# FFN output in two passes with six of eleven pairs by seven products, and retention's queries by seven products

## Chip, core and metric

The kernel runs on one core of one Trainium2 chip. Its time is the device time of one execution in microseconds, over 3 runs: median 1178.73, lowest 1178.39, highest 1178.78. The engines are named as in the profile: PE (TensorE matmul), PEld (its weight load), DVE (VectorE), ACT (ScalarE), POOL (GpSimd), SP (SyncE, which issues most transfers).

## What is computed

One decoder layer on 512 tokens and 16 meta tokens, width 1024: normalisation, a combined projection, retention (4 heads) beside stick-breaking attention (16 heads), an output projection, and a SwiGLU FFN of 2816 columns. The change is in the queries of retention and in the last product of the FFN. The core of the reference there:

```python
proj = hn @ w_in
rq, rk, rv, rg, sq, sk, sv, ga, gb = jnp.split(proj, ..., axis=-1)
q_r = rotary(heads(rq, RET_HEADS), pos) * (RET_DK ** -0.5)
k_r = rotary(heads(rk, RET_HEADS), pos)
...
def swiglu(hn, w_ffn_in, w_ffn_out):
    a, b = jnp.split(hn @ w_ffn_in, 2, axis=-1)
    return (jax.nn.silu(a) * b) @ w_ffn_out
...
ff = swiglu(rmsnorm(h, norm_ffn_pre[l]), w_ffn_in[l], w_ffn_out[l])
h = h + rmsnorm(ff, norm_ffn_post[l])
return h[:, N_META:]
```

## The kernel before

**Products in three parts.** Every fp32 matrix is split into a high part (fp32r, made by ACT) and a low part (what the high part leaves, by DVE): `split` (L104, L101). A product of matrices is then three matmuls, high by high, high by low, low by high. A weight block comes from HBM into a `raw` tile (4 of them), and its two parts into `wh` and `wl` tiles (5 each, used in rotation).

**Seven products.** Much of the kernel multiplies 2x2 blocks of matrices by seven block products instead of eight (Strassen's scheme in Winograd's form): `PRODUCTS` names them a11, a12, a22 and s1 to s4 for the weights' blocks and their sums, b11 to b22 and t1 to t4 for the activations'. POOL makes the sums into `st` tiles (2 of them), `seven` runs the products and puts them together from the banks of PSUM. FFN-in (up to 1050.9 us) does so: per pair of row blocks of the FFN's 22 it runs 168 matmuls of 256 columns.

**Retention** (335 to 745 us) goes head by head. `ret_qk(h)` loads the head's 256 query columns as two units, computes the queries by 2 x 8 x 3 = 48 matmuls of 512 columns into two banks, rotates them (DVE reads the banks, ACT and DVE split the results), then loads and computes the keys with 96 matmuls of 264 columns. Scores, values and the state follow.

**FFN-out** (from 1050.9 us) multiplies the gated activations `gt`, which stand in SBUF as 11 pairs (`gt[:, f2]`, each four blocks of 256), with `w_ffn_out`. For each of 22 row blocks it splits 512 columns of `gt` and 1024 of the weights, and for each of 4 token tiles and 2 column halves runs three matmuls of 512 columns into one of 8 banks: 528 in all. The last four row blocks (`REST`) are run token tile by token tile, in the written order (`pinned`). So a token tile ends early: its squares (ACT), the power (POOL), the scaling and the last addition (DVE) and its transfers go beside the next tile's matmuls, and only the last tile's stand behind the last matmul. FFN-out's sums per bank stay in PSUM through all 22 row blocks.

**Order.** The instructions of an engine run in the order in which a list scheduler put them, at build time, by its own costs and the order of the code; matmuls and transfers under `pinned` stay as written. A tile that is used again waits until its last reader is done.

## Time and profile before

| what | value |
|---|---|
| median of the runs | 1178.73 us (1178.39 to 1178.78) |
| the profiled execution | 1178.72 us |
| its span | 1176.9 us |
| granted clock of PE | 0.999 |
| busy: PE, DVE, ACT, POOL | 99%, 72%, 45%, 28% |
| POOL in FFN-out up to 1149 us | 0 of 95 us |

The profile is of one execution. Busy time is the union of an engine's instructions; PE counts as busy through stretches in which matmuls follow each other at their spacing, which is shorter than the time that a row gives for one of them (they overlap). The spacing is read from the chain of waits, which gives stretches of one kind with their length and number. "L95 x24" is 24 instructions of line 95. `128x256` is partitions by elements.

### The profile page before, as it was taken

To read this page: it belongs to the slowest core of one execution; us is meant where nothing else is said; L and a number is where in the kernel's file an instruction comes from. 1 tells how busy PE (TensorE), PEld (TensorE's weight loads), DVE (VectorE), ACT (ScalarE), POOL (GpSimd) and SP (SyncE) were. 2 spreads that over 40 slices of the span, in tenths; PEclk is the share of its full clock that TensorE was granted. 3 is DMA by queue.
4 is the path that set the end of the run, shared out by engine and by line. 5 is a ranking of instruction groups with operands and counts; after the bars stand their busy time and mean duration, and the time that the engine had idled before them with its cause. 6 is when DMAs were issued, how large, how long until landed. Compare 5 with 4: busy or idle time off the path is not lost.

```text
span 1176.9 us, 18856 instructions
## 1 busy us (share of the span) xinstructions
PE 1164.9 (99%) x7529; PEld 1056.3 (90%) x7529; DVE 844.0 (72%) x1120; ACT 532.1 (45%) x899; POOL 333.5 (28%) x358
## 2 busy tenths in 40 slices
PE   9999999999999999999999999999999999999997
PEld 7988999988899998998899898888999999998886
DVE  7488888888577873786586567767799998773333
ACT  6476666666233434434243334335455444442321
POOL 2021112126644403320240200001356676610000
PEclk9999999999999999999999999999999999999999
DMA  7332122222641323115122434344033333353311
GB/s 235 99 99 74 62 72 64 77 77 92 194 148 60 93 90 114 55 53 154 36 82 82 133 90 134 126 160 126 19 108 108 109 108 108 108 162 101 97 36 72
DMA packets 146536, 118.25 MB, mean 100 GB/s; under 512 B 3832, under 2 KB 135168, under 8 KB 146448
## 3 DMA queue, kind: packets, MB, share of 16 engines
q1 hardware_dynamic: 145856, 115.85, 32.5%
q8 instruction: 59, 0.97, 0.4%
q10 hardware_dynamic: 592, 1.20, 0.3%
q14 instruction: 29, 0.24, 0.1%
HBM read 109.96 MB, written 7.08 MB: 99 GB/s over the span
## 4 chain that ended last, share of the span: by engine, by line
PE 92%; DVE 5%; issue 1%; ACT 1%; DMA 0%; POOL 0%; POOLq 0%; DVEq 0%; ACTq 0%
PE pp L95 41%; PE pb L95 20%; PE pa L95 20%; PE pc L95 5%; PE px L95 3%; PE pb L98 3%; DVE wl L101 1%; DVE sm L603 1%; ACT wh L104 1%; DVE sl L101 0%; DMA ysb<-in_x_dram 0%; DVE al L101 0%; DVE kl L101 0%; DVE qb L101 0%; DVE qa L101 0%
## 5 line engine op out<-in xcount | busy, mean ns | idle before, releaser
L101 DVE TENSOR_TENSOR wl<-raw,wh 128x1024 fp32r<-128x1024 f32 x196 | 260.7, 1338 | 60.3 <-ACT wh L104 59.3
L104 ACT ACTIVATE wh<-raw 128x1024 fp32r<-128x1024 f32 x194 | 195.2, 1014 | 203.4 <-PE pa L95 59.5
L95 PE MATMUL pp<-hT,wh 128*128 128x512 f32 (+1 forms) x304 | 112.0, 369 | 0.0
L95 PE MATMUL pp<-hL,wh 128*128 128x512 f32 (+1 forms) x304 | 107.7, 354 | 0.0
L95 PE MATMUL pp<-hT,wl 128*128 128x512 f32 (+1 forms) x304 | 107.6, 354 | 0.0
L258 POOL TENSOR_TENSOR st<-raw 128x512 f32<-128x512 f32 x28 | 44.4, 1608 | 170.3 <-DMA raw<-in_w_in_dram 170.3
L101 DVE TENSOR_TENSOR wl<-st,wh 128x1024 fp32r<-128x1024 f32 x54 | 75.1, 1392 | 13.1 <-ACT wh L104 12.1
L95 PE MATMUL pp<-qk,wh 128*128 128x512 f32 x256 | 80.1, 394 | 0.0
L230 POOL TENSOR_TENSOR st<-raw 128x512 f32<-128x512 f32 x40 | 61.1, 1528 | 50.3 <-DVE wl L101 50.3
L95 PE MATMUL pp<-wh,hT 128*128 128x256 f32 (+1 forms) x240 | 73.9, 309 | 0.1
L95 PE MATMUL pp<-wl,hT 128*128 128x256 f32 (+1 forms) x240 | 73.0, 305 | 0.7 <-DVE wl L101 0.4
L95 PE MATMUL pp<-wh,hL 128*128 128x256 f32 (+1 forms) x240 | 73.0, 305 | 0.2 <-DVE hL L101 0.2
L104 ACT ACTIVATE wh<-st 128x1024 fp32r<-128x1024 f32 x54 | 56.6, 1056 | 35.6 <-PE pp L95 15.6
L95 PE MATMUL pa<-hL,wh 128*128 128x264 f32 (+1 forms) x208 | 66.2, 318 | 0.0
L95 PE MATMUL pa<-hT,wh 128*128 128x264 f32 (+1 forms) x208 | 66.2, 318 | 0.0
L95 PE MATMUL pa<-hT,wl 128*128 128x264 f32 (+1 forms) x208 | 66.1, 318 | 0.0
L603 DVE TENSOR_TENSOR_SCAN sm<-sm,mask 128x528 f32<-128x528 f32 (+1 forms) x64 | 54.8, 857 | 14.3 <-ACT sm L600 13.5
L95 PEld LDWEIGHTS pp<-hT,wl 128*128 128x128 f32 x304 | 57.2, 188 | 8.4
L613 POOL CAST mg<-sp 128x32 fp32r<-128x32 f32 x32 | 7.5, 233 | 197.6 <-DVE sp L604 153.7
L95 PEld LDWEIGHTS pp<-hT,wh 128*128 128x128 f32 x304 | 57.3, 188 | 5.8
L95 PEld LDWEIGHTS pp<-hL,wh 128*128 128x128 f32 x304 | 57.4, 189 | 5.3
L95 PEld LDWEIGHTS pp<-qk,wh 128*128 128x128 f32 x256 | 47.7, 188 | 10.7
(346 smaller groups left out, 3680.3 us busy)
## 6 DMA issues: line engine op xcount, KB each, us to landing
raw<-in_w_in_dram SPq DMA_DIRECT2D x88, 512.0 KB, 4.2
raw<-in_w_ffn_in_dram SPq DMA_DIRECT2D x44, 512.0 KB, 3.8
raw<-in_w_ffn_out_dram SPq DMA_DIRECT2D x22, 512.0 KB, 3.6
raw<-in_w_ret_out_dram SPq DMA_DIRECT2D x16, 512.0 KB, 3.4
raw<-in_w_sb_out_dram SPq DMA_DIRECT2D x8, 512.0 KB, 3.9
raw<-in_w_out_dram SPq DMA_DIRECT2D x8, 512.0 KB, 4.0
ysb<-in_x_dram SPq DMA_DIRECT2D x4, 512.0 KB, 7.1
gb_d<-go SPq DMA_DIRECT2D x8, 256.0 KB, 2.0
```

The lines of the kernel that those rows point to most:

```text
L95: return keep(nc.tensor.matmul(*args, **kw))
L98: return keep(nc.tensor.transpose(dst, src, idn))
L101: return nc.vector.tensor_tensor(lo, src, hi.bitcast(F32), op=ALU.subtract)
L104: ins = nc.scalar.activation(hi, src, AF.Copy)
L230: ins = nc.gpsimd.tensor_tensor(d, p, q, op=op)
L258: nc.gpsimd.tensor_tensor(d[:, k : k + 2], p[:, k : k + 2], q[:, k : k + 2], op=op)
L603: nc.vector.tensor_tensor_scan(rev, rev, mask[:, r0:][:, ::-1], 0.0, op0=ALU.mult, op1=ALU.max)
L613: nc.gpsimd.tensor_copy(g[:, two, 0:NM], m)
```

## The change

**Retention's queries.** `feat_quarters` loads the head's query weights in quarters and makes four sums of 512 columns on POOL; `feat_chain` runs seven products of 4 x 3 matmuls with 256 columns. Products that are only added up are chained in one bank: a11, s2, s3, a22 in the first, s1, s4 in the second, a12 in the third, with copies by ACT in between. The keys of the first half stand between the products. The result lies in SBUF, from where `rotate` reads it now.

**FFN-out.** It runs in two passes, one for each half of the 1024 output columns, and in steps `n` = 0 to 21: 0 to 10 are pass 0 with the pairs 0 to 10, 11 to 21 are pass 1 with the pairs 10, 9, 8, 7, 6, 5, 4, 3, 1, 2, 0. An odd pair is plain: 24 matmuls of 512 columns in a step. An even pair goes by seven products, 7 x 2 x 3 = 42 matmuls of 256 columns. `prepare(n)` loads a 256x512 weight block; for a seven pair POOL makes four sums of weights and three of activations, 256 columns each (and once per pair the difference t1 in place of b12), and ACT and DVE split raw weights and activations (1024 columns each), sums of weights and sums of activations (768 each). Pairs 10 and 8 keep their split activations for pass 1. The banks are put together into `y` after pass 0 (`combine`) and after pass 1. At the end the two seven pairs n=20 and 21 are run product by product, with the plain n=19 around them.

```diff
--- before.py
+++ after.py
@@ -139,13 +139,13 @@
...
-    def feat_mm(dst, unit, xh, xl, kn=KD):
+    def feat_mm(dst, unit, xh, xl, kn=KD, first=True, **kw):
...
+            mm(dst, wh[:, k, :], xh(k), start=(first and k == 0), stop=False, **kw)
+            mm(dst, wh[:, k, :], xl(k), start=False, stop=False, **kw)
+            mm(dst, wl[:, k, :], xh(k), start=False, stop=(k == kn - 1), **kw)
...
+    def feat_chain(u, tok, q, u22, beside=None):
...
+        def product(name, bank, more=False):
+            a, b = name
+            feat_mm(banks[bank], u[a], *tok.operand(b), KH, first=not more, skip_group_check=True)
...
+        def add(d, p):
+            nc.vector.tensor_tensor(d, p, d, op=ALU.add)
...
+        (q11, q12), (q21, q22) = [[q[:, e, H * t : H * (t + 1)] for t in range(2)] for e in range(2)]
+        def rest():
+            banks["c"] = bank_p()[:, :H]
+            product(("a12", "b21"), "c")
+            add(q11, banks["c"])
+        banks["a"] = bank_a()[:, 0, :H]
+        product(("a11", "b11"), "a")
+        nc.scalar.activation(q11, banks["a"], AF.Copy)
+        if beside:
+            rest()
+        banks["b"] = bank_p()[:, :H]
+        product(("s1", "t1"), "b")
+        nc.scalar.activation(q22, banks["b"], AF.Copy)
+        product(("s2", "t2"), "a", True)
+        nc.scalar.activation(q12, banks["a"], AF.Copy)
+        product(("s4", "b22"), "b", True)
+        add(q12, banks["b"])
+        product(("s3", "t3"), "a", True)
+        nc.scalar.activation(u22, banks["a"], AF.Copy)
+        add(q22, u22)
+        (beside or rest)()
+        product(("a22", "t4"), "a", True)
+        nc.scalar.activation(q21, banks["a"], AF.Copy)
...
     def ret_qk(h):
-        uq = feat_units(w_in[:, O_RQ + DK * h : O_RQ + DK * (h + 1)])
-        pq = bank_a()
-        for e in range(2):
-            feat_mm(pq[:, e, :], uq[e], xtok, ltok)
+        uq = feat_quarters(w_in[:, O_RQ + DK * h : O_RQ + DK * (h + 1)], s4, s1_first=True)
+        uk = feat_units(w_in[:, O_RK + DK * h : O_RK + DK * (h + 1)])
+        pks = []
...
+        def keys(e):
+            pk = bank_a()
+            pks.append(pk[:, :, :264])
+            for i in range(2):
+                cs = slice(264 * i, 264 * (i + 1))
+                feat_mm(pk[:, i, :264], uk[e], lambda k: hT[:, k, cs], lambda k: hL[:, k, cs])
+        pq = s4.tile([P, 4, 512], F32, tag="ub", name="ub", bufs=1)
+        feat_chain(uq, tokens, pq, pq[:, 2, :H], lambda: keys(0))
...
+        keys(1)
...
-    NPF, REST = NF // 2, 4
+    NPF, REST = NF // 2, 2
...
+    plain = lambda f2: f2 % 2 == 1
+    def pair_of(n):
+        return n if n < NPF else (10, 9, 8, 7, 6, 5, 4, 3, 1, 2, 0)[n - NPF]
+    rooms4 = [(gp, "go"), (tn, "th"), (tn, "tl")]
...
+    def prepare(n, sums):
+        g, f2 = n // NPF, pair_of(n)
+        raw = raw_of(w_ffn_out[2 * P * f2 : 2 * P * (f2 + 1), 512 * g : 512 * (g + 1)])
+        A11, A21 = raw[:, 0, 0:256], raw[:, 0, 256:512]
+        A12, A22 = raw[:, 1, 0:256], raw[:, 1, 256:512]
+        seven_, kept = not plain(f2), g == 1 and f2 >= NPF - 4
+        if seven_:
+            w = sums.tile([P, 4, H], F32, tag="st", name="st")[:, 0:3, :]
+            S2, S3, S4 = w[:, 0, :], w[:, 1, :], w[:, 2, :]
+            todo = [(gt[:, f2, 1, :], gt[:, f2, 1, :], gt[:, f2, 0, :], ALU.subtract)] if g == 0 else []
+            todo += [(S3, A11, A21, ALU.subtract), (A21, A21, A22, ALU.add), (S2, A21, A11, ALU.subtract), (S4, A12, S2, ALU.subtract)]
+            if not kept:
+                t = sums.tile([P, 4, H], F32, tag="st", name="st")[:, 0:3, :]
+                T2, T3, T4 = t[:, 0, :], t[:, 1, :], t[:, 2, :]
+                B11, T1, B21, B22 = [gt[:, f2, q, :] for q in range(4)]
+                todo += [(T2, B22, T1, ALU.subtract), (T3, T2, B11, ALU.subtract), (T4, B21, T2, ALU.subtract)]
+            for d, p, q, op in todo:
+                nc.gpsimd.tensor_tensor(d, p, q, op=op)
+        wh, wl = wun_split(raw.rearrange("p k (c n) -> p (k c) n", c=2))
+        ws[n] = {k: (wh[:, v], wl[:, v]) for k, v in dict(a11=0, s1=1, a12=2, a22=3).items()}
+        ws[n]["rows"] = [[v[:, 2 * k : 2 * k + 2].rearrange("p c n -> p (c n)") for v in (wh, wl)] for k in range(2)]
+        if kept:
+            ops[n] = ops[pair_of(n)]
+        else:
+            place, name = rooms4[pair_of(n) % 4]
+            if g:
+                place, name = rooms4[(2, 1, 0, 3)[(n - NPF) % 4]]
+            o = place.tile([P, 4, KH, H], F32R, name=name, bufs=1).rearrange("p a b n -> p (a b) n")
+            split(o[:, 0:4], o[:, 8:12], gt[:, f2])
+            ops[n] = {k: (o[:, v], o[:, 8 + v]) for k, v in dict(b11=0, t1=1, b12=1, b21=2, b22=3, t2=4, t3=5, t4=6).items()}
+        if seven_:
+            wh, wl = wun_split(w)
+            ws[n].update({k: (wh[:, v], wl[:, v]) for k, v in dict(s2=0, s3=1, s4=2).items()})
+            if not kept:
+                split(o[:, 4:7], o[:, 12:15], t)
...
+        for n in range(2):
+            prepare(n, sst)
...
-    ps_ac.close()
...
+        ys = [s8.tile([P, 4, 512], F32, name="y", bufs=2) for _ in range(2)]
...
+        names = ["a11", "s2", "s1", "s3", "s4", "a12", "a22"]
+        pairs = dict(PRODUCTS)
+        both_of, single, banks, keys, begun = {}, {}, {}, {}, set()
+        def new_banks():
+            begun.clear()
+            for a, room in zip(names, (bank_p, bank_p, bank_b, bank_b)):
+                v = room()
+                banks[a], keys[a], single[a] = [v[:, 0:256], v[:, 256:512]], [a, a], v
+            for t, two in enumerate((("a12", "a22"), ("s4", "x22"))):
+                both_of[t] = bank_a()
+                for c, a in enumerate(two):
+                    banks[a], keys[a] = [both_of[t][:, s, 256 * c : 256 * (c + 1)] for s in range(2)], [(t, 0), (t, 1)]
+            both_of["a12"], both_of["a22"] = [both_of[0][:, :, 256 * c : 256 * (c + 1)] for c in range(2)]
+            both_of["s4"], both_of["x22"] = [both_of[1][:, :, 256 * c : 256 * (c + 1)] for c in range(2)]
...
+        def three(d, key, x, w):
+            mm(d, x[0], w[0], start=key not in begun, stop=False, skip_group_check=True)
+            begun.add(key)
+            mm(d, x[0], w[1], start=False, stop=False, skip_group_check=True)
+            mm(d, x[1], w[0], start=False, stop=True, skip_group_check=True)
...
+        def product(n, a, parts=(0, 1)):
+            for s in parts:
+                three(banks[a][s], keys[a][s], tile_of(n, pairs[a], s), ws[n][a])
+        def plain_products(n, tokens_=(0, 1)):
+            for t in tokens_:
+                for s in range(2):
+                    for k in range(2):
+                        three(both_of[t][:, s, :], (t, s), tile_of(n, f"b{k + 1}{t + 1}", s), ws[n]["rows"][k])
+        def step(n):
+            if plain(pair_of(n)):
+                plain_products(n)
+            else:
+                for a in names:
+                    product(n, a)
...
+        def combine(y, a):
+            q11, q21, q12, q22 = [y[:, q, :].rearrange("p (s n) -> p s n", s=2) for q in range(4)]
+            p = both_of[a] if a in both_of else whole(a)
+            if a == "x22":
+                nc.scalar.activation(q22, p, AF.Copy)
+            elif a == "a11":
+                nc.scalar.activation(q11, p, AF.Copy)
+            elif a == "s2":
+                add(q21, p, q11)
+            elif a == "s1":
+                add(q12, p, q21)
+                add(q22, q12, q22)
+            elif a == "s3":
+                add(q22, p, q22)
+                add(q21, p, q21)
+            elif a == "s4":
+                add(q12, p, q12)
+            elif a == "a12":
+                add(q11, p, q11)
+            else:
+                add(q21, p, q21)
...
+        def scaled(i, g, cn):
+            v, w = columns(ys[g], i, g, cn)
+            (nc.gpsimd if g and i > 1 else nc.vector).tensor_tensor(v, v, w, op=ALU.mult)
...
+        def finish(i, n):
+            rs = s8.tile([P, 1], F32, tag="rs", name="rs", bufs=NT)
+            nc.vector.scalar_tensor_tensor(rs, sc[i][0], 1e-6, sc[i][n - 1], op0=ALU.add, op1=ALU.add)
+            nc.gpsimd.tensor_tensor(rs, rs, nhalf, op=ALU.pow)
+            for g in range(2):
+                v, _ = columns(ys[g], i, g, both)
+                cs = slice(512 * g, 512 * (g + 1))
+                h = h2[:, i, cs].rearrange("p (c n) -> p c n", c=2)
+                if g or i == 1:
+                    nc.vector.scalar_tensor_tensor(v, v, rs, h, op0=ALU.mult, op1=ALU.add)
+                else:
+                    nc.scalar.activation(v, v, AF.Copy, scale=rs)
+                    nc.gpsimd.tensor_tensor(v, v, h, op=ALU.add)
+                queue = nc.scalar if i == 1 and g else nc.sync
+                queue.dma_start(out[i * P : (i + 1) * P, cs].rearrange("p (c n) -> p c n", c=2), v)
...
+        order = ["x22"] + names
+        new_banks()
+        last = 2 * NPF - REST - 1
+        for n in range(last):
+            if n >= 2:
+                prepare(n, s8)
+            if n == NPF:
+                for a in order:
+                    combine(ys[0], a)
+                new_banks()
+            if NPF + 2 <= n < NPF + 2 + NT:
+                squares(n - NPF - 2, 0, both, sc[n - NPF - 2][0])
+                scaled(n - NPF - 2, 0, both)
+            step(n)
+        for n in range(last, 2 * NPF):
+            prepare(n, s8)
...
+        plain_products(last, (1,))
+        for a in names:
+            if a == "a22":
...
+                plain_products(last, (0,))
+                combine(ys[1], "a12")
+                combine(ys[1], "a22")
+            for parts in ((0, 1),) if a != "a22" else ((0,), (1,)):
+                if a == "a22":
+                    i = parts[0]
+                    banks[a][i], keys[a][i] = bank_p()[:, 0:256], ("last", i)
+                for n in range(last + 1, 2 * NPF):
+                    product(n, a, parts)
+                if a == "a22":
+                    cs = slice(256 * i, 256 * (i + 1))
+                    add(ys[1][:, 1, cs], banks[a][i], ys[1][:, 1, cs])
+                    if i == 0:
+                        for e in range(2):
+                            squares(e, 1, slice(0, 1), sc[e][1])
+                            scaled(e, 1, slice(0, 1))
+                            nc.gpsimd.tensor_tensor(sc[e][0], sc[e][0], sc[e][1], op=ALU.add)
+                    squares(i, 1, slice(1, 2), sc[i][2])
+                    scaled(i, 1, slice(1, 2))
+                    finish(i, 3)
+            if a == "a11":
+                combine(ys[1], "x22")
+            if a[0] == "s" or a == "a11":
+                combine(ys[1], a)
+            if a == "s4":
+                for i in (2, 3):
+                    squares(i, 1, both, sc[i][1])
+                    scaled(i, 1, both)
+                for i in (2, 3):
+                    finish(i, 2)
```

Three places in the order of the instructions (the names are tiles: `gt` the gated activations, `st` sums, `wh`/`wl` and `go`/`th`/`tl`/`o4` the split parts of weights and activations, `y` results, the number at the end tells tiles apart).

POOL, where FFN-in ends and FFN-out begins; before:

```order
279 L230 TENSOR_TENSOR st_11203<-raw_11199,raw_11201 128x512
280 L230 TENSOR_TENSOR st_11204<-raw_11199,st_11203 128x512
281 L1341 TENSOR_TENSOR rs_12121<-rs_12121,nhalf_78 128x1
282 L1341 TENSOR_TENSOR rs_12161<-rs_12161,nhalf_78 128x1
283 L1341 TENSOR_TENSOR rs_12201<-rs_12201,nhalf_78 128x1
```

The same place now, the seven sums of n=4:

```order
317 L1336 TENSOR_TENSOR st_11891<-raw_11889 128x256
318 L1336 TENSOR_TENSOR raw_11889<-raw_11889 128x256
319 L1336 TENSOR_TENSOR st_11892<-gt_9211 128x256
320 L1336 TENSOR_TENSOR st_11891<-raw_11889 128x256
321 L1336 TENSOR_TENSOR st_11892<-st_11892,gt_9211 128x256
322 L1336 TENSOR_TENSOR st_11892<-gt_9211,st_11892 128x256
323 L1336 TENSOR_TENSOR st_11891<-raw_11889,st_11891 128x256
```

Where POOL had only the four powers of the last step, it has seven sums for each seven pair now.

DVE at the boundary of the passes now (n=10's last splits, n=11's, n=12's, then the banks of pass 0; before, such a place does not exist):

```order
1082 L101 TENSOR_TENSOR tl_12205<-st_12192,tl_12205 128x768
1083 L101 TENSOR_TENSOR wl_12209<-st_12191,wh_12208 128x768
1084 L101 TENSOR_TENSOR wl_12264<-raw_12256,wh_12263 128x1024
1085 L101 TENSOR_TENSOR wl_12268<-st_12258,wh_12267 128x768
1086 L101 TENSOR_TENSOR wl_12332<-raw_12329,wh_12331 128x1024
1087 L1428 TENSOR_TENSOR y_11715<-pp_11718,y_11715 128x512
1088 L1428 TENSOR_TENSOR y_11715<-pb_11719,y_11715 128x512
1089 L1428 TENSOR_TENSOR y_11715<-y_11715 128x512
1090 L1428 TENSOR_TENSOR y_11715<-pa_11721,y_11715 128x512
1091 L1428 TENSOR_TENSOR y_11715<-pb_11720,y_11715 128x512 x2
1092 L1428 TENSOR_TENSOR y_11715<-pa_11722,y_11715 128x512
```

The additions that empty the banks (`pp_11718` is s2's, `pb_11719` s1's, `pb_11720` s3's) stand behind three splits of weights for n=11 and n=12.

POOL at the end now (before, it had the powers of rows 281 to 284 alone):

```order
381 L1468 TENSOR_TENSOR y_11716<-y_11716,gfin_11701 128x2x256
382 L1475 TENSOR_TENSOR rs_12799<-rs_12799,nhalf_78 128x1
383 L1468 TENSOR_TENSOR y_11716<-y_11716,gfin_11701 128x2x256
384 L1475 TENSOR_TENSOR rs_12807<-rs_12807,nhalf_78 128x1
385 L1484 TENSOR_TENSOR y_11715<-y_11715,h2_8491 128x2x256
386 L1526 TENSOR_TENSOR sc_11703<-sc_11703,sc_11704 128x1
387 L1526 TENSOR_TENSOR sc_11707<-sc_11707,sc_11708 128x1
388 L1484 TENSOR_TENSOR y_11715<-y_11715,h2_8491 128x2x256
389 L1475 TENSOR_TENSOR rs_12860<-rs_12860,nhalf_78 128x1
390 L1475 TENSOR_TENSOR rs_12879<-rs_12879,nhalf_78 128x1
391 L1484 TENSOR_TENSOR y_11715<-y_11715,h2_8491 128x2x256
```

Scaling, powers and three of the last additions of the four token tiles stand in one row on POOL.

89 lines of the change are left out of this document (25 added, 64 removed).

## The prediction

> **What bounds the kernel now.** I read the page's busy table and chain of waits first, then TensorE's own waits, then the windows of the stages that the change touches. The page:
>
> ```profile
> span 1176.9 us, 18856 instructions
> PE 1164.9 (99%) x7529; PEld 1056.3 (90%) x7529; DVE 844.0 (72%) x1120; ACT 532.1 (45%) x899; POOL 333.5 (28%) x358
> PE 92%; DVE 5%; issue 1%; ACT 1%; DMA 0%; POOL 0%; POOLq 0%; DVEq 0%; ACTq 0%
> ```
>
> TensorE is busy for 99% of the span, and 92% of the chain that ended last is matmuls. TensorE's waits between 330 and 1170 us, which hold retention and both FFN products, are these two rows and no others:
>
> ```profile
> PE pa L95 <- ACT nT L104: 0.2, 1, 0.2
> PE pa L95 <- DVE nL L101: 0.2, 1, 0.2
> ```
>
> So time is saved only by taking matmul time away, and lost only where TensorE begins to wait, or after its last matmul. The price of a matmul is its spacing, which the chain gives as stretches (start, length, how many):
>
> ```profile
> 355.46 16.96 PE pa L95 x96
> 373.72 5.84 PE pa L95 x48
> 872.11 2.86 PE pb L95 x24
> 1053.57 2.72 PE pc L95 x12
> 1154.43 5.44 PE pb L95 x24
> ```
>
> The first is one head's queries and keys together: 48 of 512 columns and 48 of 264. The second is 48 of 264 alone. The queries of a head thus take 16.96 - 5.84 = 11.12 us, 0.2317 us each. The third is FFN-in by seven products, 256 columns: 2.86 / 24 = 0.1192. The last two are FFN-out now: 0.2267 for 512 columns.
>
> Three windows (us; busy time of PE, PEld, DVE, ACT, POOL): a head of retention, FFN-in, FFN-out:
>
> ```profile
> 466.00:571.00 105.00, 104.92 (x694) 95.78 (x693) 73.33 (x94) 38.11 (x51) 25.82 (x20) 1.00 0.29 88
> 850.00:1048.00 198.00, 198.00 (x1662) 198.00 (x1661) 177.03 (x176) 95.34 (x119) 122.59 (x75) 1.00 0.37 108
> 1054.00:1149.00 95.00, 95.00 (x421) 78.67 (x420) 32.69 (x34) 26.37 (x33) 0.00 (x0) 1.00 0.26 81
> ```
>
> FFN-out has two thirds of VectorE's time free and POOL idle. FFN-in is the stage nearest to what FFN-out becomes: VectorE 89% busy, POOL 62%, and TensorE without a gap.
>
> **Queries.** Per head 48 matmuls of 512 columns go and 7 x 4 x 3 = 84 of 256 come: 84 x 0.1192 = 10.01 against 11.12, so -1.11 a head, **-4.4** for four. Beside them come four POOL sums, one and a half more split units, five ACT copies and three VectorE additions a head; prices are in these groups (mean ns) and, for POOL, minimum/median/maximum:
>
> ```profile
> L269 ACT ACTIVATE ub<-pp 128x256 f32<-128x256 f32 x20 | 7.5, 375 | 22.7 <-DVE gt L1283 22.7
> L277 DVE TENSOR_TENSOR ub<-pp,ub 128x256 f32<-128x256 f32 x20 | 8.5, 423 | 1.8
> L104 ACT ACTIVATE wh<-st 128x1024 fp32r<-128x1024 f32 x54 | 56.6, 1056 | 35.6 <-PE pp L95 15.6
> L230 POOL TENSOR_TENSOR st<-st,raw x20: 1282/1296/1622, 829.5 to 1029.2; 128x512 f32<-128x512 f32 x20
> L196 POOL TENSOR_TENSOR ts<-hT x8: 732/748/1602, 275.7 to 320.1; 128x256 f32<-128x256 f32 x8
> ```
>
> That is 4 x 1.29 = 5.2 us on POOL, 5 x 0.375 + 1.5 x 1.06 = 3.5 on ACT, and 3 x 0.42 + 1.5 x 1.22 = 3.1 on VectorE, in a head of 105 us where these engines have 79, 67 and 32 us free. I cost it at nothing: the keys of half zero stand between the products while banks are copied, and TensorE's 104.92 of 105.00 covers the rest. With that cover gone a head loses up to what it gained, so the bounds are -4.4 and 0.
>
> **FFN-out's matmuls.** 528 of 512 columns (119.7 us by 0.2267) become 2 x 5 x 24 = 240 of 512 and 2 x 6 x 42 = 504 of 256: 54.4 + 60.1 = 114.5, so **-5.2**. If the wide ones fall back to the queries' 0.2317 it is -4.0.
>
> **What feeds them.** A seven pair asks POOL for seven sums of 256 columns (four of weights, three of activations), 7 x 0.74 = 5.2 us, and VectorE for the low halves of raw weights, operands (1024 each), weight sums and token sums (768 each). VectorE's prices, and what they become beside POOL, are in FFN-in's window, by shape:
>
> ```profile
> L101 DVE TENSOR_TENSOR wl<-st,wh 128x1024 fp32r<-128x1024 f32 x39 | 54.5, 1396 | 11.1 <-ACT wh L104 10.1 <-PE pb L95 0.8
> L101 DVE TENSOR_TENSOR wl<-raw,wh 128x1024 fp32r<-128x1024 f32 x22 | 41.4, 1880 | 3.1 <-ACT wh L104 3.1
> L101 DVE TENSOR_TENSOR wl<-raw,wh 128x512 fp32r<-128x512 f32 x20 | 23.8, 1192 | 4.0 <-ACT wh L104 4.0
> L1283 DVE TENSOR_TENSOR gt<-ub 128x1024 f32<-128x1024 f32 x9 | 14.0, 1557 | 0.3
> L274 DVE TENSOR_TENSOR ub<-pb,ub 128x512 f32<-128x512 f32 x20 | 13.6, 678 | 0.0
> ```
>
> and, one by one, where POOL stopped there (start, length):
>
> ```profile
> 1030.41 1.75 POOL L230 TENSOR_TENSOR st<-raw 128x512 f32<-128x512 f32 x1
> 1032.12 2.28 POOL L230 TENSOR_TENSOR st<-raw,st 128x512 f32<-128x512 f32 x1
> 1031.77 1.48 DVE L1283 TENSOR_TENSOR gt<-ub 128x1024 f32<-128x1024 f32 x1
> 1033.18 2.31 DVE L101 TENSOR_TENSOR wl<-raw,wh 128x1024 fp32r<-128x1024 f32 x1
> 1042.08 1.22 DVE L101 TENSOR_TENSOR wl<-raw,wh 128x1024 fp32r<-128x1024 f32 x1 [0.33 <-ACT wh L104]
> ```
>
> Alone the split takes 1.22 and POOL's sum 1.29. From 1031.77 to POOL's end at 1034.40 both run, 2.63 us, and they lose 0.26 + 1.09 on VectorE and 0.46 + 0.99 on POOL, 2.8 us: side by side, these two hardly gain on one after the other. The row that reads a bank (L274) keeps its 0.68. Over the window POOL lost 122.59 - 75 x 1.29 = 25.8 us and VectorE's two-SBUF operations some 35 (133.7 in the four rows against 61 x 1.22 + 20 x 0.68 + 9 x 1.22 = 99.0). I therefore add up both engines' SBUF work as if it went through one door, with a discount of 0 to 15% of the time in which both run.
>
> [...]
>
> From TensorE's entry into FFN-out to the last seven pair of pass 0 the door has: five seven pairs x 5.2 = 25.9 of POOL; VectorE 5 x (2 x 1.22 + 2 x 0.95) + 4 x 2.44 + 1.22 = 32.7 (0.95 for 768 columns is an estimate between 0.68 and 1.22). Together 58.6. TensorE takes 5.44 + 5.01 = 10.45 for a plain and a seven pair, reaches n=10 after 52.3 and its first product of sums some 3 us later: 55.3. With the discount on 45 us of overlap the door needs 51.9, without it 58.6: TensorE waits between 0 and 3.3 us, and the way POOL to ACT to VectorE and back to POOL through two `st` buffers adds up to 2. FFN-in carried 99 + 97 = 196 us of such work in 198 without one wait; here it is 58.6 in 55.3. Nearer the lower end: **+1.5** (0 to 5).
>
> **The boundary of the passes.** Pass 1 wants its banks at once, and eight VectorE additions (seven of 0.68 from banks, 4.8 us) and two ACT copies free them, behind three weight splits (3 x 1.1) in VectorE's order. The bank of s3 is wanted 2.15 us after n=10's last matmul and is read sixth. If VectorE comes to the additions 2 us before that matmul's end nothing is late; two us later, 2 us are. **+1** (0 to 2).
>
> **The last two seven pairs** (n=20, 21) stand back to back. From the end of n=16 TensorE has 5.44 + 5.01 + 2.72 = 13.2 us of other work. In it n=20's four splits (4.3 us behind the first ACT copy), then n=21's sums on POOL, which need n=20's `st` buffers (5.2 us, beside VectorE nearer 7), then ACT 0.85 + VectorE 0.95 have to fit: about 14 us, against a first use 2.1 after the 13.2. **+1** (0 to 3).
>
> **After the last matmul.** Before:
>
> ```profile
> 1170.36 0.39 PE L95 MATMUL pc<-wh,gl 128*128 128x512 f32 x1
> 1170.85 0.60 ACT L1337 ACTIVATE sq<-pc 128x512 f32<-128x512 f32 x1 [2.03 <-PE pc L95]
> 1172.39 1.54 DVE L1346 SCALAR_TENSOR_TENSOR fo<-fo,rs,h 128x512 f32<-128x512 f32 x3
> L1341 POOL TENSOR_TENSOR rs<-rs,nhalf 128x1 f32<-128x1 f32 x4 | 2.2, 552 | 135.7 <-DVE rs L1340 135.7
> ```
>
> With its spacing the last matmul is done at 1170.59; VectorE ends at 1173.93 and the span 2.97 later, 6.31 us after the matmuls. In the change POOL's queue decides: from the bank of s4 on, which is complete 1.43 + 2.72 + 1.43 = 5.6 us before the end, it has five operations of 512 columns (6.5 us), four powers (2.2) and two additions of one column (at most 1.1). It starts 1 us after the bank, at -4.6, and is through at +5.1 alone, or at +6.9 when it loses 1.8 to VectorE's scaling and last additions (some 5 us, half of it beside POOL). With 2.97 behind it: 9.8 against 6.31, **+3.5** (1.8 to 5).
>
> **Sum:** -4.4 - 5.2 + 1.5 + 1 + 1 + 3.5 = -2.6 against the profiled execution's 1178.72, which stands 0.01 under the median of the runs and 1.82 over its span: **1176.1 us**.
>
> **Rivals.** First, slower: POOL and VectorE exclude each other wholly, and feeding, not TensorE, sets pass 0. Then 3.3 + 1.3 there, 2 at the boundary and 3 at the last pairs, 9.6 instead of 3.5: +3.5, **1182.2**. It decides once the door's work outruns 55.3 us, so with a discount under 3.3 of the 45 us that overlap. For it: the rows at 1030 to 1034. Against: TensorE's 198.00 of 198.00 beside 196 us of the same work.
>
> Second, clean: the splits of operands, which only need the gate, run ahead into free room, no wait above 0.5 appears anywhere, and POOL's tail is little disturbed (+2.5): -4.4 - 5.2 + 0.5 + 2.5 = -6.6, **1172.1**. For it speaks the empty FFN-out window (VectorE 32.69 of 95, POOL 0); against it that 10.45 us of TensorE face 12 us of clean door work.
>
> Third, the queries bring nothing: banks are copied between products on ACT while another head's splits stand ahead, and each head waits 1.1 us: 1176.1 + 4.4 = **1180.5**. For it: seven products need banks back at once. Against: VectorE has 32 of 105 us free, and POOL 79.
>
> **How the numbers follow.** The forecast's case, 1174 to 1178.5, has 0.50; the first rival 0.20, the second 0.20, the third 0.10. About 0.2%, 2.3 us, is what can be told from no change: faster is below 1176.4, slower above 1181.1. The forecast's case gives 0.29 faster and 0.21 same; the first rival 0.17 slower and 0.03 same; the second 0.20 faster; the third 0.07 same and 0.03 slower. So 0.49, 0.31, 0.20. The range takes in most of both outer rivals: 1171.5 to 1183.
>
> **What would show it.** Queries: 84 matmuls a head in 10.0 us, and the keys of both halves with no more idle time on TensorE than now. FFN-out: 114.5 us of matmul spacing, and waits of TensorE there of 3.5 us, on splits of sums. POOL's 256-column sums at 0.74 alone, well over 1 beside VectorE. The last transfer issued 6.9 us after the last matmul, from POOL's final addition. Waits above 7 us in FFN-out speak for the first rival, below 1 for the second; idle time of over 1 us a head between 330 and 750 us for the third. A spacing of 256 columns other than 0.119 would make all of it wrong.

## The result, and the profile after

The changed kernel takes 1194.1 us in the median (1192.92 to 1194.92, 4 runs), the one before 1178.76 beside it (1178.39 to 1178.86): a ratio of 1.013, with a 95% interval of 1.0112 to 1.0148. Forecast were 1176.1 us and a range to 1183. The profiled execution took 1194.79 us. From its page:

```profile
span 1193.0 us, 19838 instructions
PE 1162.7 (97%) x7889; PEld 1069.4 (90%) x7889; DVE 933.0 (78%) x1172; ACT 573.5 (48%) x956; POOL 476.7 (40%) x465
PE 69%; DVE 14%; POOL 7%; issue 5%; ACT 3%; DMA 2%; DVEq 0%; POOLq 0%; ACTq 0%
```

TensorE's busy time fell by 2.2 us and the span grew by 16.1. Matmuls are 69% of the chain that ended last, where they were 92%; VectorE, POOL and ACT have 24% of it. The first and the last matmul of FFN-out in the trace:

```profile
1056.92 0.28 PE L95 MATMUL pp<-wh,go 128*128 128x256 f32 x1
1181.53 0.28 PE L95 MATMUL pp<-wh,go 128*128 128x256 f32 x1
```

Three stretches add up to the 16.1 us:

| stretch | before | after | difference | forecast |
|---|---|---|---|---|
| up to FFN-out's first matmul | 1050.88 | 1056.92 | +6.0 | -4.4 |
| FFN-out, first to last matmul done | 119.7 | 124.7 | +5.0 | -1.7 |
| from there to the end of the span | 6.31 | 11.35 | +5.0 | +3.5 |

All three are worse than forecast, the first by 10.4 us. Where TensorE waited (engine and line, for what; total us, times, longest):

```profile
PE pp L95 <- DVE acc L1153: 2.1, 2, 1.1
PE pb L95 <- DVE y L1428: 1.8, 1, 1.8
PE pb L95 <- DVE qk L101: 1.7, 1, 1.7
...
PE pp L95 <- DVE wl L101: 1.5, 3, 0.7
PE pp L95 <- DVE y L1428: 1.5, 1, 1.5
...
PE pp L95 <- ACT wh L104: 1.3, 3, 0.6
PE pa L95 <- DVE wl L101: 1.1, 1, 1.1
PE pp L95 <- ACT y L1440: 0.9, 1, 0.9
PE pa L95 <- DVE rt L1025: 0.9, 1, 0.9
```

Most is for VectorE, some for ACT. `acc`, `qk`, `rt` and the `wl` of the row `PE pa` are retention's, `y` is the boundary of the passes. The other `wl` row and the `wh` row stand for two waits each in FFN-out and one before it. Retention's window, first of the kernel before, then of the changed one (PE, PEld, DVE, ACT, POOL):

```profile
345.00:750.00 405.00, 404.79 (x2649) 368.37 (x2648) 290.23 (x375) 154.93 (x207) 94.27 (x72) 1.00 0.32 96
```

```profile
345.00:750.00 405.00, 397.97 (x2769) 368.73 (x2769) 322.83 (x388) 166.53 (x232) 125.87 (x88) 1.00 0.30 93
```

VectorE is busy for 33 us more and TensorE idle for 7. (Of the 10.4 us by which this stretch missed its forecast, the busy figure shows these 7: a matmul's row, 0.28 us for 256 columns, is longer than its spacing of 0.12, so it covers short gaps.) How one of these waits comes about, in the second head (start, length):

```profile
443.17 3.81 POOL L230 TENSOR_TENSOR st<-raw 128x512 f32<-128x512 f32 x2 [21.21 <-DMA raw<-in_w_in_dram]
446.94 1.74 POOL L230 TENSOR_TENSOR st<-st,raw 128x512 f32<-128x512 f32 x1
448.76 1.62 POOL L230 TENSOR_TENSOR st<-raw,st 128x512 f32<-128x512 f32 x1
445.74 3.48 DVE L101 TENSOR_TENSOR vl<-ub,vh 128x512 fp32r<-128x512 f32 x2
449.15 2.31 DVE L101 TENSOR_TENSOR wl<-raw,wh 128x1024 fp32r<-128x1024 f32 x1
```

POOL's four sums for the queries' weights run just beside splits of VectorE. Two `vl` of 512 columns take 3.48 us instead of 1.36 (0.68 for one alone), and the queries' own low half, which stands behind them and beside POOL's last sum, 2.31 instead of 1.22. It ends at 451.46, and TensorE waits 1.1 us for it (the row `PE pa L95 <- DVE wl L101` above).

### The profile page after: what moved, and what is told of

Read it like the earlier page. It is cut to its first block, busy times and chain, and to the rows that moved or that the text cites. A ratio compares the mean times of both kernels' runs of the same rounds, so it can differ in the third digit from the quotient of the medians.

```text
span 1193.0 us, 19838 instructions
## 1 busy us (share of the span) xinstructions
PE 1162.7 (97%) x7889; PEld 1069.4 (90%) x7889; DVE 933.0 (78%) x1172; ACT 573.5 (48%) x956; POOL 476.7 (40%) x465
## 4 chain that ended last, share of the span: by engine, by line
PE 69%; DVE 14%; POOL 7%; issue 5%; ACT 3%; DMA 2%; DVEq 0%; POOLq 0%; ACTq 0%
PE pp L95 34%; PE pb L95 16%; PE pa L95 13%; DVE wl L101 5%; POOL st L1336 4%; PE px L95 3%; PE pb L98 3%; ACT wh L104 1%; DMA raw<-in_w_in_dram 1%; POOL raw L1336 1%; DVE sm L646 1%; DVE vl L101 1%; POOL st L230 1%; DVE y L1428 1%; POOL ts L196 1%
## 5 line engine op out<-in xcount | busy, mean ns | idle before, releaser
L101 DVE TENSOR_TENSOR wl<-raw,wh 128x1024 fp32r<-128x1024 f32 x196 | 276.1, 1416 | 50.8 <-ACT wh L104 48.7
L101 DVE TENSOR_TENSOR wl<-st,wh 128x1024 fp32r<-128x1024 f32 (+1 forms) x74 | 103.3, 1400 | 23.1 <-ACT wh L104 22.8
L95 PE MATMUL pp<-hT,wh 128*128 128x512 f32 (+2 forms) x336 | 120.8, 360 | 0.0
L230 POOL TENSOR_TENSOR st<-raw 128x512 f32<-128x512 f32 x48 | 73.7, 1539 | 112.2 <-DMA raw<-in_w_in_dram 71.4
L95 PE MATMUL pp<-hT,wl 128*128 128x512 f32 (+2 forms) x336 | 116.6, 347 | 0.0
L95 PE MATMUL pp<-hL,wh 128*128 128x512 f32 (+2 forms) x336 | 116.5, 347 | 0.0
L104 ACT ACTIVATE wh<-st 128x1024 fp32r<-128x1024 f32 (+1 forms) x74 | 75.5, 1022 | 63.5 <-PE pp L95 28.7
L95 PE MATMUL pp<-qk,wh 128*128 128x512 f32 x256 | 80.9, 396 | 2.4 <-DVE acc L1153 2.1
L263 POOL TENSOR_TENSOR st<-raw 128x512 f32<-128x512 f32 x28 | 45.1, 1630 | 73.2 <-DMA raw<-in_w_in_dram 51.1
L95 PE MATMUL pp<-wl,hT 128*128 128x256 f32 (+1 forms) x240 | 73.3, 306 | 0.7 <-DVE wl L101 0.4
L95 PE MATMUL pp<-wh,hT 128*128 128x256 f32 (+1 forms) x240 | 73.7, 308 | 0.1
L95 PE MATMUL pp<-wh,hL 128*128 128x256 f32 (+1 forms) x240 | 73.0, 304 | 0.2 <-DVE hL L101 0.2
L95 PEld LDWEIGHTS pp<-hT,wl 128*128 128x128 f32 x336 | 63.2, 188 | 8.3
L95 PEld LDWEIGHTS pp<-hT,wh 128*128 128x128 f32 x336 | 63.3, 188 | 5.8
L95 PEld LDWEIGHTS pp<-hL,wh 128*128 128x128 f32 x336 | 63.4, 189 | 5.3
L95 PE MATMUL pa<-wh,th 128*128 128x256 f32 (+1 forms) x216 | 64.5, 327 | 0.0
L95 PEld LDWEIGHTS pp<-qk,wh 128*128 128x128 f32 x256 | 46.8, 188 | 12.8 <-DVE acc L1153 2.5
L95 PE MATMUL pa<-wh,tl 128*128 128x256 f32 (+1 forms) x204 | 54.3, 296 | 0.0
L95 PE MATMUL pa<-wl,th 128*128 128x256 f32 (+1 forms) x172 | 53.1, 309 | 0.0
```

Source lines behind the costliest of these rows:

```text
L95: return keep(nc.tensor.matmul(*args, **kw))
L101: return nc.vector.tensor_tensor(lo, src, hi.bitcast(F32), op=ALU.subtract)
L104: ins = nc.scalar.activation(hi, src, AF.Copy)
L230: ins = nc.gpsimd.tensor_tensor(d, p, q, op=op)
L263: nc.gpsimd.tensor_tensor(d[:, k : k + 2], p[:, k : k + 2], q[:, k : k + 2], op=op)
```

## Experiments: the two parts

The change taken apart: `e1_queries` is the kernel before with the new `ret_qk`, `feat_chain` and `feat_quarters`; `e2_ffn` is the changed kernel with the old `ret_qk`.

> Only the queries' part of the change, FFN-out as before. In the changed kernel FFN-out begins 6.04 us later than before (1056.92 against 1050.88), so if the two parts don't touch each other this takes 1178.8 + 6.0 = 1184.8 us, whatever the cause inside retention. Under 1181 would mean that the queries' loss needs the FFN's part (another order of the instructions ahead of it).

> Only FFN-out's part, retention's queries as before. From FFN-out's first matmul to the last the changed kernel takes 124.7 us against 119.7, and 11.35 us against 6.31 behind the last: +10.1, so 1188.8 us if the parts don't touch each other. The forecast's own sum for this part was -5.2 + 3.5 + 3.5 = +1.8, 1180.6.

Measured: 1185.5 us (ratio 1.0058, 1.0043 to 1.0073) and 1188.26 (1.0083, 1.0068 to 1.0098), against 1178.69. That is +6.8 and +9.6, together 16.4 where the whole change had +15.3. The parts hardly touch each other, and each can be studied alone.

## Experiments: the queries

First POOL's sums left out (`e3_nosums`: the loop over the four sums is empty, and the raw weights stand in for `x` and `y`), and made by VectorE (`e4_qdve`):

```diff
-            ins = nc.gpsimd.tensor_tensor(d, p, q, op=op)
+            ins = (nc.vector if s1_first else nc.gpsimd).tensor_tensor(d, p, q, op=op)
```

> The queries' part alone, without POOL's four sums a head: the split units that held sums are filled from the raw weights, the same splits, matmuls, copies and rotation remain; the sums are left out of the computation, so the queries are not the model's. Theory (POOL's sums stretch VectorE's splits beside them, and these arrive late at TensorE): most of the 10.4 us comes back, 1175 to 1178 us. Rival (the chain of products: its banks, its copies and a rotation that can only start after the last product): little changes, 1183 to 1185. Rival (more splits on VectorE, whoever makes the sums): 1181 to 1185.

> The queries' part alone, with its four sums a head made by VectorE in place of POOL: 4 x 0.68 = 2.7 us more of VectorE a head and no contention from them. Theory (contention): the splits of the queries' units are back at 1.22 and about half to all of the loss comes back, 1176 to 1181 us. Rival (VectorE is simply given too much work and stands late in its queue): slower than with POOL, above 1185.

Without sums 1179.7 us (ratio 1.0008, 0.9998 to 1.0019): 5.8 us come back, less than the theory asked. With the sums on VectorE 1182.37 (1.0032, 1.002 to 1.0043): 3.1 us come back although VectorE does more. That is 1.4 us above the theory's range and 2.6 below the rival's bound. (Leaving sums out takes away two things at once, POOL's work beside VectorE and the wait of a split for its sum; with the sums on VectorE the second stays in part.) Even without sums, 5.4 us against the matmuls' own saving stayed open: 1179.7 against 1174.3. Three runs looked for them in the wrong place. The keys behind the products instead of between them:

```diff
-        feat_chain(uq, tokens, pq, pq[:, 2, :H], lambda: keys(0))
+        feat_chain(uq, tokens, pq, pq[:, 2, :H])
+        keys(0)
```

> The queries' part without POOL's sums, as in the run before (1179.7 us), but with both halves of the keys behind the seven products instead of the first half between them. The question is the 4.6 us which that run is above the forecast's 1174.3 without any sums. If they come from the rotation of the queries, which can only start after the last product and now stands close before that of the keys: TensorE's waits on the rotation (0.3 to 0.6 us a head) go, 1177.5 to 1178.5. If the products wait for their banks to be copied, now that nothing stands between them: slower, 1181 to 1186.

The split units cut back to the two of the kernel before:

```diff
-            c, b = wun_split(y), wun_split(x)
+            b = c = wun_split(x)
+            d = tuple(v[:, 0:KH, :] for v in a)
...
-        d = wun_split(A22)
+        d = d if s1_first else wun_split(A22)
```

> The queries' part without POOL's sums (1179.7 us) and now also without the one and a half more split units: two units are split as before and used in place of all seven operands, so the queries are not the model's. Theory (what is left of the queries' loss, 5 us against the 1174.3 that 84 narrow matmuls alone would give, is VectorE's and ACT's work for more units): 1175 to 1176.5. Rival (it is the chain itself, its copies and additions and the late rotation): 1178.5 to 1180.

And the kernel before, with wide products, in the new arrangement:

```diff
+        feat_mm(p0, uq[0], xtok, ltok)
+        nc.scalar.activation(pq[:, 0, :], p0, AF.Copy)
+        keys(0)
+        p1 = bank_p()
+        feat_mm(p1, uq[1], xtok, ltok)
+        nc.scalar.activation(pq[:, 1, :], p1, AF.Copy)
...
+        keys(1)
```

> The kernel before, with 48 wide matmuls a head for the queries, but in the arrangement of the change: the first feature half, then the keys' first half, then the second feature half, each copied by ACT into SBUF, and the rotation of the queries read from there, between the halves of the keys. No sums, no more split units, no chain of products. Without POOL's sums the narrow queries had stayed 5 us above their matmul time. Theory (that rest is the late rotation from SBUF, which stands just ahead of the keys' rotation on VectorE and ACT): this kernel loses about the same against the one before, 1182 to 1184 us. Rival (it comes from the chain of seven products, its copies and additions): 1178.5 to 1179.5 us.

1179.62, 1181.03 and 1178.15 us (ratios 1.0011, 1.0019 and 0.9994; the last one's interval is 0.9984 to 1.0003). The first lies between the two forecasts for it, the second 1.0 us above the slower one, the third 0.4 under the one without a loss. The order of the keys is worth nothing, fewer splits bring nothing, a late rotation costs nothing by itself. What the trace of `e10_nosplits` did show is POOL's other work in retention, the sums of the gate's products (L267 there), meeting the rotation:

```profile
488.62 3.98 POOL L267 TENSOR_TENSOR st<-raw 128x512 f32<-128x512 f32 x2 [7.35 <-DVE rt L1030]
489.64 1.79 DVE L1027 TENSOR_TENSOR rt<-rt 128x528 f32<-128x528 f32 x1
493.60 1.79 DVE L101 TENSOR_TENSOR qk<-rt,qk 128x528 fp32r<-128x528 f32 x1
```

Each of VectorE's two steps takes 0.70 in the kernel before. So the next run left the gate's sums out as well, in `tok_quarters`:

```diff
-        x = sums.tile([P, KH, 256], F32, tag="st", name="st")
-        y = sums.tile([P, KH, 256], F32, tag="st", name="st")
+        x, y = A11, A22
...
-        for d, p, q, op in ((y, A11, A21, ALU.subtract), (A21, A21, A22, ALU.add), (x, A21, A11, ALU.subtract), (A12, A12, x, ALU.subtract)):
+        for d, p, q, op in ():
```

> The queries' part without POOL's sums for the queries (1179.7 us) and now also without POOL's sums for the gate products of retention: POOL stands idle there but for the powers, the split units are filled from the raw weights, so queries and gate are not the model's. Matmuls, splits, copies, additions and rotation are those of the change. Theory (what is left are the gate's sums, which begin 488 us into the program, beside the keys' rotation, and stretch a rotation step from 0.68 to 1.8 us): 1174.3 to 1175.5 us. Rival (the chain of seven products itself, with its copies and additions): 1178 to 1180.

1173.79 us, ratio 0.9958 (0.9943 to 0.9974): 4.9 us under the kernel before, where the forecast's sum for the queries alone was -4.4. The window of retention in this run:

```profile
345.00:745.00 400.00, 400.00 (x2797) 372.74 (x2797) 286.76 (x394) 170.43 (x236) 8.99 (x16) 1.00 0.32 97
```

TensorE's busy row has no gap in 400 us, with the whole chain of products, all its copies and additions and the late rotation in place. VectorE has the splits, additions and rotation of the change to do and is busy for the same share of the time as before it (286.76 of 400 against 290.23 of 405); POOL is busy for 8.99 us where it had 94.27. So what the queries lost goes with POOL's sums, 5.8 us with its new ones and 5.9 with its old ones.

By which meeting with VectorE the old sums cost 5.9 us isn't shown. The rotation is the candidate of the rows above, but `e12_rotlate`, with wide products, has the same meeting and loses nothing (a step of its rotation and the split behind it; the figures are busy us and mean ns):

```profile
L984 DVE TENSOR_TENSOR rt<-rt 128x528 f32<-128x528 f32 x4 | 6.1, 1522 | 0.0
L101 DVE TENSOR_TENSOR qk<-rt,qk 128x528 fp32r<-128x528 f32 x8 | 8.9, 1112 | 0.0
```

In the kernel before these means are 701 and 705 ns. So a stretched rotation alone costs nothing with wide products, and no run settles what it costs with narrow ones.

Can the saving be had with all sums made? The last run of the study put every sum of retention on VectorE, beside the best end of FFN-out (below). It is `e14_dvescale` with the new `ret_qk`, and `nc.vector` for `nc.gpsimd` in `feat_quarters` (for the queries) and `tok_quarters`:

> Both parts of the change, with every sum of retention and of FFN-out made by VectorE instead of POOL, and the end of the run of 1177.0 us (plain pairs last, scaling by VectorE). In retention VectorE was busy 286.8 of 400 us without any sums; 72 sums of 512 columns at 0.68 add 49: 84%. Theory (POOL beside VectorE is the whole loss): the queries' forecast of -4.4 comes on top of 1177.0, 1172.6 to 1174.5 us, faster than both kernels. Rival (VectorE at 84% comes late in places): 1176 to 1180.

1183.97 us (ratio 1.0043, 1.003 to 1.0057), which is 9.5 us above the theory's range and 4.0 above the rival's. The rival has the direction: with 72 sums more, VectorE's splits come late again. TensorE's two largest waits in retention:

```profile
PE pa L95 <- DVE wl L101: 3.1, 3, 1.1
PE pp L95 <- ACT qk L104: 1.7, 3, 0.6
```

TensorE's granted clock was also 0.50 in two stretches of 3.4 us of this profiled execution, which took 1186.11 us (last section). The run of the five with the highest granted clock, 0.999, took 1182.91, so the stretches at 0.50 are the smaller part of the loss.

## Experiments: FFN-out

Sums by VectorE in `prepare` (`e5_ffndve`), sums left out (`e6_ffnnosums`: `pass` in that place, with `raw` and `gt` read for `w` and `t`), and four `st` buffers instead of two from n=2 on (`e8_st4`), each on `e2_ffn`; the edits of the first and the last:

```diff
-                nc.gpsimd.tensor_tensor(d, p, q, op=op)
+                nc.vector.tensor_tensor(d, p, q, op=op)
```

```diff
+    ST_BUFS = lambda pool: 2 if pool is sst else 4
...
-            w = sums.tile([P, 4, H], F32, tag="st", name="st")[:, 0:3, :]
+            w = sums.tile([P, 4, H], F32, tag="st", name="st", bufs=ST_BUFS(sums))[:, 0:3, :]
...
-                t = sums.tile([P, 4, H], F32, tag="st", name="st")[:, 0:3, :]
+                t = sums.tile([P, 4, H], F32, tag="st", name="st", bufs=ST_BUFS(sums))[:, 0:3, :]
```

> FFN-out's part alone, with the seven sums of a seven pair made by VectorE (256 columns at 0.41) in place of POOL (0.74). VectorE then has 6.78 + 2.9 = 9.7 us in the 10.45 us that TensorE takes for a plain and a seven pair, and nothing stands beside it. Theory (POOL and VectorE go through one door, 12 us against 10.45, and that makes the sums and with them the boundary late): TensorE's waits of 8.2 us in FFN-out shrink to 1 to 3, so 1181 to 1183 with the long tail still there. Rival (VectorE's own queue is the trouble, its additions at the boundary stand behind splits): no better than 1188.3, rather slower, up to 1192.

> FFN-out's part alone, without POOL's sums: the split operands of the sums are taken from the raw weights and the gate directly, so the result is not the model's; all splits, matmuls, additions and the tail stay. Theory: the waits of TensorE in pass 0, at the boundary and at the last pairs are gone but for about 1 us: 1178.7 - 5.2 + 5.0 (tail) + 1 = 1179.5 us. Rival (the additions that empty the banks come late without POOL too): waits of 3 us and more remain at the boundary, 1182 to 1184.

> FFN-out's part alone with four buffers for the sums instead of two. In its trace n=11's sums start on POOL only when n=10's weight sums have been split (VectorE ended at 1110.80 in the changed kernel, POOL began at 1110.97, after 1.95 us of idle time). Theory A (the way through two buffers makes them late): with four the sums run a pair ahead, the waits at the boundary (5.5 us) and at the last two seven pairs (1.5 us) shrink to half or less, 1182 to 1185 us. Theory B (the door's throughput): POOL only waits elsewhere and VectorE is slowed as much, 1187 to 1189.

1179.57 us (ratio 1.001, 1.0 to 1.0019), 1179.18 (1.0004, 0.9993 to 1.0014) and 1185.01 (1.0054, 1.0039 to 1.0069), against 1188.26 with POOL's sums in two buffers. The first is better than its theory asked (1181 to 1183). The same window in three of the four, in the order `e2_ffn`, `e5_ffndve`, `e6_ffnnosums`:

```profile
1052.00:1166.00 114.00, 109.19 (x681) 98.54 (x680) 89.53 (x72) 57.16 (x69) 88.80 (x71) 0.99 0.27 84
```

```profile
1052.00:1166.00 114.00, 113.79 (x733) 103.88 (x732) 99.14 (x152) 58.83 (x73) 3.56 (x4) 1.00 0.23 79
```

```profile
1052.00:1166.00 114.00, 114.00 (x737) 104.38 (x736) 76.54 (x81) 57.75 (x73) 3.64 (x4) 1.00 0.25 80
```

With the sums on VectorE its busy time is 99 us for 152 instructions; with them on POOL it is 90 for 72. POOL's 71 instructions took 89 us for what VectorE does in 23 (99.14 - 76.54). TensorE waits 0.2 us instead of 4.8 in this window, with the same splits, sums and additions. The trouble between FFN-out's first and last matmul was this pairing, and neither the number of splits nor the place of the boundary's additions. The 11.4 us behind the last matmul stay in both runs.

Four buffers take away a third of the loss, at the edge of Theory A: the boundary and the last pairs have no wait any more, but TensorE now waits 3.6 us in one piece at n=2, for a high half of weights. The stall has moved. The boundary in the changed kernel, with POOL's wait for a buffer at its head:

```profile
1110.97 1.38 POOL L1336 TENSOR_TENSOR st<-raw 128x256 f32<-128x256 f32 x1 [1.95 <-DVE tl L101]
1113.20 1.06 ACT L104 ACTIVATE wh<-raw 128x1024 fp32r<-128x1024 f32 x1 [2.56 <-POOL raw L1336]
1117.22 1.75 DVE L101 TENSOR_TENSOR wl<-raw,wh 128x1024 fp32r<-128x1024 f32 x1
1118.90 0.68 DVE L1428 TENSOR_TENSOR y<-pp,y 128x512 f32<-128x512 f32 x1
1119.63 0.39 PE L95 MATMUL pp<-wh,tl 128*128 128x256 f32 x1 [1.49 <-DVE y L1428]
1123.57 0.36 PE L95 MATMUL pb<-wh,tl 128*128 128x256 f32 x1 [1.80 <-DVE y L1428]
```

(The figure in brackets is idle time; between the starts of these matmuls the gap over the usual spacing is 1.7 and 2.0 us.) The first wait at the boundary, 1.1 us by the starts of the matmuls, is for ACT's copy of a bank. n=11's sums start when n=10's have been split; one of them is made in place, in `raw`, so even the split of the raw weights waits for POOL; VectorE's splits come late by that and are stretched (1.75, where one alone takes 1.22), and the additions that empty the banks stand behind them. That the buffer is at the root of it `e8_st4` shows, which has no wait here.

Then the end. First a different one on `e5_ffndve`: the two plain pairs 3 and 1 last, token tile by token tile, with the banks of the sums put together before (`e9_plainlast`); then the tiles in another order, with VectorE's work as written (`e11_tiles`); then the scaling on VectorE (`e14_dvescale`). The order of the pairs, the same in all three, and the loop of the last:

```diff
-        return n if n < NPF else (10, 9, 8, 7, 6, 5, 4, 3, 1, 2, 0)[n - NPF]
+        return n if n < NPF else (10, 9, 8, 7, 6, 4, 5, 2, 0, 3, 1)[n - NPF]
...
+        for i in (0, 2, 1, 3):
+            t, s = i // 2, i % 2
+            for n in range(last, 2 * NPF):
+                for k in range(2):
+                    three(both_of[t][:, s, :], (t, s), tile_of(n, f"b{k + 1}{t + 1}", s), ws[n]["rows"][k])
+            v, w = columns(ys[1], i, 1, both)
+            kept_(nc.vector.tensor_tensor(v, both_of[t][:, s, :].rearrange("p (c n) -> p c n", c=2), v, op=ALU.add))
+            squares(i, 1, both, sc[i][1])
+            if before_ is not None:
+                last_adds(before_)
+            kept_(nc.vector.tensor_tensor(v, v, w, op=ALU.mult))
...
```

> FFN-out's part alone, sums by VectorE as in the run of 1179.6 us, and another end: pass 1 runs the pairs 10, 9, 8, 7, 6, 4, 5, 2, 0 and then the two plain ones 3 and 1, token tile by token tile as the kernel before does; the banks a11, s1, s2, s3 are put together ahead of them, and each tile needs one addition from its bank, squares, scaling, power and the last additions. Theory (the 11.4 us behind the last matmul are VectorE's queue of additions and scalings for two token tiles at once): with one tile left, it is 6.31 plus 0.7 to 1.5, 7.0 to 7.8 us, so 1179.6 - 4 = 1175 to 1176 us, faster than both kernels. Rival (the two seven pairs 2 and 0 and the splits of 3 and 1 come late, or the last three tiles' work on VectorE piles up): 1177 to 1180.

> As the run of 1180.2 us (plain pairs last, sums by VectorE), with the last four token tiles in the order 0, 2, 1, 3 and VectorE's work of the end in a written order (a tile's addition from its bank ahead of the last additions of the tile before); the scaling of all tiles on POOL. In the run before TensorE waited 0.95 us twice for the addition of the tile that shares its pair of banks, and the last tile's addition started 1.7 us late, behind four last additions of other tiles. Theory (both are the order's, not the work's): 1.9 us of waits go and the end shrinks from 9.3 us to 7.5: 1176 to 1177 us. Rival (VectorE's work per tile, 2.4 us beside POOL's scaling, is too much for 2.7 us of matmuls): 1178.5 to 1180.5.

> As the run of 1178.4 us (plain pairs last, tiles 0, 2, 1, 3, written order at the end), but VectorE scales the tiles, not POOL. There POOL's scaling of 512 columns (1.7 us) held up VectorE's sum of two columns of one element, which took 1.2 us instead of 0.16, and with it the next tile's addition. Theory: VectorE's work per tile grows by 0.69 but its waits of 1.1 go, the end shrinks from 10.0 us to about 8.7: 1177.1 us. Rival (VectorE's 3 us a tile pile up against 2.7 us of matmuls): 1178.5 us or more.

1180.2 us (ratio 1.0012, 1.0003 to 1.0021), 1178.44 (0.9996, 0.9987 to 1.0005) and 1176.97 (0.9984, 0.9976 to 0.9993). The first was a miss: two waits of 0.95 us and a late last addition ate the gain. The second came out at its rival's edge: it removed the waits, but its end was 10 us, for the reason that these rows show (first POOL's scaling and VectorE's sum of one element in `e11_tiles`, then that sum in `e14_dvescale`):

```profile
1165.84 1.71 POOL L1533 TENSOR_TENSOR y<-y,gfin 128x512 f32<-128x512 f32 x1 [0.86 <-ACT sq L1462]
1166.35 1.22 DVE L1537 SCALAR_TENSOR_TENSOR rs<-sc 128x1 f32<-128x1 f32 x1
```

```profile
1166.42 0.15 DVE L1537 SCALAR_TENSOR_TENSOR rs<-sc 128x1 f32<-128x1 f32 x1
```

An operation of 0.15 us takes 1.22 where it began beside one of POOL's: it ends at 1167.57, POOL's at 1167.55. The next tile's addition stands behind it. With POOL's scaling out of the way the end is 8.3 us (forecast 8.7), and `e14_dvescale`, with wide queries, six pairs by seven products and FFN-out's sums on VectorE, is the one version of the study with nothing left out that beats both kernels by more than its interval, by 1.7 us against the one before.

## Why the prediction was wrong

Two steps failed above all. The queries' sums, splits and copies were costed at nothing, and the stretch ahead of FFN-out grew by 6.0 us instead of shrinking by 4.4. At the boundary of the passes VectorE's splits were taken as on time, and 6.6 us were lost where the sum had 1. In detail:

- **The spacings** held. 256 columns came every 0.119 to 0.120 us and 512 every 0.227 to 0.233; without waits FFN-out's matmuls took 115.1 us in `e6_ffnnosums` (1051.15 to 1166.25), forecast 114.5. The savings were real: against -4.4 for the queries `e13_nopool` has -4.9, against -5.2 for FFN-out `e6_ffnnosums` has 119.7 to 115.1, -4.6.
- **Queries, "I cost it at nothing"**: this step failed, and with it the bounds of -4.4 and 0; the part alone cost +6.8 (`e1_queries`). I compared POOL's 5.2 and VectorE's 3.1 us a head with the time that these engines have free in 105 us. What counted is what ran beside the sums: splits that TensorE waited for next (2.31 us for 1.22, and a wait of 1.1, in the second head). Nor did the loss stop at the gain, since work is delayed that has nothing to do with the queries' sums: `acc`, `vl` and the keys' rotation. The rows for it stood in the prediction, in the part on FFN-out (2.63 us side by side, 2.8 us lost); I had not applied them to retention. My third rival had the place, and the wrong cause: `e13_nopool` has the chain and its banks, and no wait.
- **What feeds FFN-out, +1.5**: measured 1.5 (0.77 + 0.51 and what follows, at 1069 and 1071 us). The size held, by luck: the sum has the door fall behind pair by pair until n=10, and the trace has both waits at n=2 and none over 0.2 us from there to the boundary.
- **The boundary, +1 (0 to 2)**: measured 6.6, the largest miss within FFN-out. I had seen that VectorE's additions stand behind three splits, and had taken the splits as on time. They were late by POOL's wait for a buffer and the sum made in place; waits of 1.1 (for ACT), 1.7 and 2.0 us (for VectorE) follow, and then 3.41 us of matmuls at a granted clock of 0.50, a loss of some 1.6 us, which was in no term.
- **The last two seven pairs, +1**: measured 1.5.
- **After the last matmul, +3.5, "POOL's queue decides"**: 5.0, and in the trace it is VectorE's queue, stretched beside POOL. The rows:

```profile
1183.83 0.74 DVE L1428 TENSOR_TENSOR y<-pp,y 128x256 f32<-128x256 f32 x2
1184.49 1.29 DVE L1468 TENSOR_TENSOR y<-y,gfin 128x256 f32<-128x256 f32 x2
1185.93 1.18 POOL L1475 TENSOR_TENSOR rs<-rs,nhalf 128x1 f32<-128x1 f32 x2 [0.77 <-DVE rs L1474]
1186.63 3.08 DVE L1481 SCALAR_TENSOR_TENSOR y<-y,rs,h 128x512 f32<-128x512 f32 x3 [0.37 <-POOL rs L1475]
1187.43 1.74 POOL L1484 TENSOR_TENSOR y<-y,h 128x512 f32<-128x512 f32 x1 [0.32 <-ACT y L1483]
```

  The addition from the last banks starts 2.2 us after the last matmul (1181.65), behind other banks' additions, a last addition and a scaling of other tiles; POOL sits idle before its powers; then three last additions, 0.75 each alone, take 3.08 beside POOL's. VectorE ends at 1189.71 and the span 3.3 us later.
- **The first rival**, one door for POOL and VectorE, had a chance of 0.20. Rows of the traces come near its door: in the kernel before 2.8 us were lost in 2.63 us side by side, and the sum of one element above, 1.22 for 0.15, ends 0.02 us after POOL's operation. That feeding sets pass 0 they don't show, with 1.5 us of waits there where it had 4.6. Its 9.6 us of waits in FFN-out equal the 9.6 found by luck: it had 4.6 + 2 + 3, the trace has 1.5 + 6.6 + 1.5, with some 1.6 lost at the clock of 0.50 among them. It also went into the sum for FFN-out alone. The queries add to its 1182.2 the 4.4 us that were not saved and the 6.8 that they cost, 1193.4, near the 1194.1 measured, which is in part the same luck. The 198 of 198 us of TensorE in FFN-in, which I held against the rival, can go together with such a door, if the work ahead of TensorE is deep enough there; no run tests that reading.

## What to carry to other kernels

Before work is given to POOL, look at which splits and sums of VectorE from SBUF will run beside it and who waits for them: in the changed kernel's FFN-out the splits of raw weights (1024 columns) took 1.60 us in the mean where one alone takes 1.22, while additions of 512 columns that read a bank took 0.68 to 0.69 as alone. Here FFN-out's sums were cheaper on VectorE (23 us against 89 on POOL), and with retention's sums added VectorE's splits came late again. Free time of an engine over a stage told little where TensorE waited for the very next split: POOL had 311 of retention's 405 us free in the kernel before, and the queries cost 6.8 us. A saving in matmuls of under 1% has to be held against the end of the kernel too, which cost 5.0 us here, more than the 4.6 that FFN-out's matmuls saved.
